# S5's moves between partitions as DMAs, and retention's rotary exchange as a product, in a two-layer hybrid trunk

## The chip, the cores and the metric

The kernel runs on one core of a Trainium2 chip. Its time is the device time of one execution in microseconds. Three runs of the kernel before gave 1293.81 us in the median (1292.19 to 1296.15). The engines are called PE (TensorE), DVE (VectorE), ACT (ScalarE), POOL (GpSimd) and SP (SyncE).

## The reference, cut to what matters

The trunk has two layers. Each normalises the 272 tokens (16 meta tokens and 256 of the input, width 1024), multiplies them by one wide matrix `w_in`, and gives slices of the product to four mixers (retention, S5, SSD, HGRN2). Sigmoid gates merge them; an output projection and a squared-ReLU MLP follow. Two pieces matter here.

```python
def rotary(x):                      # retention's q and k, four heads of 64 channels
    cos, sin = ...                  # angles by token and channel
    x1, x2 = x[..., :half], x[..., half:]
    return jnp.concatenate([x1 * cos - x2 * sin, x1 * sin + x2 * cos], axis=-1)

def s5_mixer(u, ...):               # 32 groups of 16 channels, 64 complex states a group
    uf = u.reshape(bsz, t, S5_GROUPS, S5_GROUP)
    bu_re, bu_im = ...              # group by group, uf times B
    _, _, xr, xi = lax.associative_scan(combine, (a_re, a_im, bu_re, bu_im), axis=1)
    y = ...                         # group by group, real part of C x
    y = y.reshape(bsz, t, BRANCH_WIDTH) + d_skip * u
    y = jax.nn.gelu(y)
    a, gt = jnp.split(y @ glu_w + glu_b, 2, axis=-1)
    return a * jax.nn.sigmoid(gt)
```

## The kernel before

Activations lie with the features on the partitions, as tiles of [128, k, 272 tokens]. The weights come in 336 chunks of 128x1024 float32 (512 KB), in the order of their use, and each chunk is used once. SP loads a chunk (`wst`, L318, three buffers); ACT makes its high part `whi` (L325, three buffers) and DVE the rest, `wlo` (L327, two buffers), both in the float32r format. PE then adds 24 products per chunk (`gemm`, L344, L345 and L347): high weights by high activations, high by low, low by high. So PE can't begin a chunk before ACT, nor finish it before DVE.

Beside that, the engines do the mixers' own work, and the order on each engine is written when the program is built, by a scheduler that simulates the program and picks by ranks of urgency; loads and cuts of chunks rank well ahead of their place. A change to one part therefore moves instructions elsewhere. The order on an engine is fixed at run time: an instruction that waits holds all that stand behind it.

S5 takes its input from four products `proj` in `s5_in`, 128 channels by 272 tokens each. Its states want another layout: 4 interleaved strands of tokens by 32 channels (two groups) on the partitions, and 68 steps along the free dimension. ACT first takes each product out of PSUM into `early` (L1060), and then 16 copies move blocks of 32 partitions by 4x68 elements from one group of 32 partitions to another: odd quadrants on DVE (L1067), even ones on ACT (L1069). `s5_run` does four pairs of groups at a time, four times a layer: products (L1101), rotation and scans on DVE and POOL (L1107 to L1129), products again (L1135, L1138), and the sum Y (L1140). After the second and the fourth of them `s5_out` applies gelu (L1146) and moves half of the channels back in 16 copies of 32x136 (L1152 on DVE, L1154 on ACT). "Half of S5" below means two such passes and their `s5_out`. At the end of `s5` the split into high and low parts follows (L362 on ACT, L364 on DVE).

The passes of S5 stand among the chunks that other mixers need: the first half of layer 0 ends near chunk 51, the second near chunk 58; in layer 1 near chunks 216 and 224. Retention's `ret_in` runs in the same places: q and k out of PSUM (L1475), the tables of cosine and sine loaded in two pieces (L276), then on POOL four multiplications of 32 partitions each that write to the neighbouring 32 (L1482), one of all 128 (L1483), and two adds (L1486, L1487). Values come out in L1492.

Names: `mb`, `mc`, `ma` and `g` are PSUM banks, `S` places in SBUF handed on, `s5a` to `s5g` the S5 parameters in the making (L1003 to L1051), `cst` the constants.

Of the kernel before, what the change touches and what calls it, by code (L numbers as in the profile page):

```python
# [23 lines left out]
# column offsets of w_in  # L24
# [5 lines left out]
# ---------------------------------------------------------------- chunk order  # L30
# One chunk: [128 rows of the contraction, 8 * 128 columns].
# [28 lines left out]
# ---------------------------------------------------------------- small parameters  # L60
# [11 lines left out]
for _name, _w in (("ident", 128), ("ones", 128), ("cen", 128), ("m432", 432), ("he", 1), ("ho", 1), ("le", 1), ("lo", 1),  # L72
                  ("rh", 1), ("rl", 1), ("r1", 1)):
    CONSTS[_name] = (_n, _w)
    _n += _w
# [3 lines left out]
NST, NHI, NLO = 3, 3, 2  # weight chunks in flight: as loaded, high parts, low parts  # L79
PD, PS = 1500, 400  # how far ahead of their place loads and cuts of chunks rank  # L80
HN, FP = 3000, 3000  # ranks of the head norms' scales and of what fills the norms' waits
RES_DVE, RES_END = 6, 6  # tiles of a residual that VectorE takes; the others are GpSimd's
RES_PE = ("mb", "mb", "mc")  # banks of the last residual's tiles that TensorE sums
STORE = ((3, 5), (6, 8), (5, 6))  # the last residual's other tiles, as they are stored
HOLD = 2  # the chunk after a norm whose cut waits for the norm
OK = 4  # from this k on the second column tile waits for the first
HL, EH = (2, 3), (3, 4)  # chunks of a layer's start whose low, high parts wait for the norm's scale
AK, WARM = 5, 14  # where the first norm's sums come in the second chunk; products before the first
LH, LO, LU = (2,), (2,), (2,)  # chunks after a norm that take their low parts last
# [4 lines left out]
def shape_constants():  # L94
# [10 lines left out]
    put("cen", np.eye(128) - 1.0 / 128)  # L105
    t = np.arange(T)
# [6 lines left out]
    # rows of the log-decays, 16 a head: 0..5 for the high parts, 6..11 for the low parts, the other factor being 1 or 0  # L113
# [15 lines left out]
    # rotary tables with the decay of retention: [128, (c | s), (q0 q1 k0 k1), t]  # L129
# [4 lines left out]
    for i in range(2):  # L134
        for q in range(4):
# [3 lines left out]
            for k in range(2):  # L139
                g = (1.0 / up) * 64 ** -0.5 if k else up  # L140
                rot[rows, 0, 2 * k + i] = np.cos(ang).T * g
                # this row feeds the other half: the first half goes to x1*sin, the second to -x2*sin
                sgn = 1.0 if q % 2 == 0 else -1.0
                rot[rows, 1, 2 * k + i] = sgn * np.sin(ang).T * g
# [10 lines left out]
def layout(inp):  # L155
    """Every array the program reads, laid out for it; values only move."""
# [52 lines left out]
    # [layer, (g p), quarter, (b_re b_im c_re c_im), pair, (g j)], zero where the two groups differ  # L209
# [24 lines left out]
class Net:  # L234
# [27 lines left out]
    # ---- small helpers  # L262
    def slot(self, k, shape, dt=F32):
        """one of the 4352-byte places; each is handed on in program order"""
# [7 lines left out]
    def load_after(self, out, in_, dep):  # L272
        """a load that takes its tile only when dep is there"""
# [28 lines left out]
    def behind(self, *key):  # L302
        """a chunk's parts may have to wait their turn on an engine"""
        return self.tc.issue_after(self.hold[key].ins) if key in self.hold else nullcontext()

    # ---- weights: each chunk comes in float32 and is cut into two float32r parts, exactly
# [26 lines left out]
    def gemm(self, out, w, wk, x, xk, n, start=True, stop=True, after=None, late=False):  # L333
        """out += sum over k of W[wk + k]^T x[xk + k], the three products of the parts that count;
        from k = after[0] on behind the instruction after[1]; with late the weights' low part comes last"""
# [23 lines left out]
    def split(self, src, hi, lo, scale=1.0):  # L359
        """hi + lo == scale * src, both float32r."""  # L360
# [15 lines left out]
    def tables(self, name):  # L376
        """the activation tables of what follows, ahead of it"""
        self.tc.keep_in_program_order(self.nc.scalar.preload_act_table_set(name))

    # ---- one layer  # L380
# [4 lines left out]
    def run(self):  # L385
# [4 lines left out]
        # keys, padded with zeros to three tiles of 128 tokens  # L390
# [4 lines left out]
        # the array's clock comes up while the first loads are under way  # L395
# [6 lines left out]
    def layer(self, l):  # L402
# [7 lines left out]
        # ---- pre-mix norm: the first products take h * w as it is, and the norm's scale after them  # L410
# [45 lines left out]
        if not last:  # L456
            # parameters of the next layer's S5, for what the norms leave idle
# [12 lines left out]
        # ---- out projection  # L470
# [15 lines left out]
        # ---- MLP; its input norm's scale s goes into the output's norm: m s^2 / sqrt(mean(m^2 s^4) + eps)  # L486
        # is m / sqrt(mean(m^2) + eps s^-4), and each partition carries its part of the second term
# [36 lines left out]
    def pre_tiles(self, l, wname, sl, big):  # L524
        """h * w, cut in two, as tiles; what makes them and sums the squares of h; and the sums"""
# [34 lines left out]
    def sums_of(self, l, wname, N, mm, extra=None):  # L560
        """products of 8 column tiles, scaled by the norm's weight; and on every partition the sum of their squares"""
# [23 lines left out]
    def fill(self, f):  # L585
        """products between the sums of a norm and what needs it"""
# [3 lines left out]
    def residual(self, mw, ps, sl, fs, eps=True):  # L590
        """h += mw / rms, and what comes next of each tile"""
# [11 lines left out]
        if fs is None:  # L603
            # some of the sums are the tensor engine's, which has h before the norm is there
# [930 lines left out]
```

## Time and profile before

| | |
|---|---|
| median of three runs | 1293.81 us |
| the profiled execution's span | 1294.5 us |
| PE busy | 1231.3 us (95%) |
| DVE busy | 898.3 us (69%) |
| ACT busy | 695.2 us (54%) |
| POOL busy | 388.4 us (30%) |
| DMA | 186.69 MB, 144 GB/s |

PE's share of 95% is the mean over stages that differ: the norms, and the stretch around layer 0's S5, hold most of the idle time. A row of a timeline gives the start in us, the duration, and in brackets how long the engine was idle before and who released it. Two rows may overlap by some tens of ns, since an instruction starts while the one before it drains.

### The profile page before, as it was taken

To read this page: it belongs to the slowest core of one execution; us is meant where nothing else is said; L and a number is where in the kernel's file an instruction comes from. 1 tells how busy PE (TensorE), PEld (TensorE's weight loads), DVE (VectorE), ACT (ScalarE), POOL (GpSimd) and SP (SyncE) were. 2 spreads that over 40 slices of the span, in tenths; PEclk is the share of its full clock that TensorE was granted. 3 is DMA by queue.
4 is the path that set the end of the run, shared out by engine and by line. 5 is a ranking of instruction groups with operands and counts; after the bars stand their busy time and mean duration, and the time that the engine had idled before them with its cause. 6 is when DMAs were issued, how large, how long until landed. Compare 5 with 4: busy or idle time off the path is not lost.

```text
span 1294.5 us, 24278 instructions
## 1 busy us (share of the span) xinstructions
PE 1231.3 (95%) x9534; PEld 1185.8 (92%) x9534; DVE 898.3 (69%) x1480; ACT 695.2 (54%) x1218; POOL 388.4 (30%) x416
## 2 busy tenths in 40 slices
PE   9999998986999989999989999998999998999997
PEld 8989888885999989999988999998999997999996
DVE  8999958987555775554459795689865486655444
ACT  6446755533465466554445548546536456665442
POOL 2332336686100332210015241265680031322001
PEclk9999999997999999999999999998999999999999
DMA  6423332341345435445443332442343554455552
GB/s 238 154 84 114 112 125 94 103 140 65 115 169 174 172 110 183 172 178 175 170 145 131 121 128 83 154 142 92 115 160 131 188 181 153 153 189 183 188 184 98
DMA packets 53187, 186.69 MB, mean 144 GB/s; under 512 B 6096, under 2 KB 7248, under 8 KB 53072
## 3 DMA queue, kind: packets, MB, share of 16 engines
q1 hardware_dynamic: 50480, 179.40, 40.1%
q10 hardware_dynamic: 2592, 5.74, 1.3%
q8 instruction: 75, 1.23, 0.4%
q14 instruction: 40, 0.33, 0.1%
HBM read 184.06 MB, written 1.05 MB: 143 GB/s over the span
## 4 chain that ended last, share of the span: by engine, by line
PE 70%; DVE 17%; POOL 5%; issue 5%; ACT 2%; DMA 1%; DVEq 0%; SPq 0%; ACTq 0%; POOLq 0%
PE g L347 21%; PE g L345 21%; PE g L344 21%; DVE wlo L327 4%; DMA s5a<-in_bc 1%; DVE S L1152 1%; PE mb L711 1%; POOL S L1482 1%; PE mb L717 1%; DVE S L1395 1%; DVE s5a L1004 1%; DVE h L600 1%; DVE S L1262 1%; PE ma L711 1%; PE ma L717 1%
## 5 line engine op out<-in xcount | busy, mean ns | idle before, releaser
L327 DVE TENSOR_TENSOR wlo<-wst,whi 128x1024 fp32r<-128x1024 f32 x336 | 434.5, 1294 | 244.0 <-PE g L347 209.8
L325 ACT ACTIVATE whi<-wst 128x1024 fp32r<-128x1024 f32 x336 | 355.6, 1059 | 368.8 <-PE g L345 285.4
L347 PE MATMUL g<-xh_u,wlo 128*128 128x272 f32 (+1 forms) x1024 | 301.7, 296 | 16.5 <-DVE wlo L327 16.4
L344 PE MATMUL g<-xh_u,whi 128*128 128x272 f32 (+1 forms) x1024 | 300.3, 294 | 1.3 <-ACT S L654 0.9
L345 PE MATMUL g<-xl_u,whi 128*128 128x272 f32 (+1 forms) x1024 | 298.1, 292 | 0.0
L344 PE MATMUL g<-S,whi 128*128 128x272 f32 (+1 forms) x832 | 236.1, 288 | 4.2 <-ACT S L537 3.7
L347 PE MATMUL g<-S,wlo 128*128 128x272 f32 (+1 forms) x808 | 230.5, 289 | 1.8 <-DVE wlo L327 1.8
L345 PE MATMUL g<-S,whi 128*128 128x272 f32 (+1 forms) x768 | 220.4, 289 | 3.1 <-DVE S L548 3.1
L347 PEld LDWEIGHTS g<-xh_u,wlo 128*128 128x128 f32 x1024 | 196.3, 192 | 20.8 <-DVE wlo L327 18.7
L344 PEld LDWEIGHTS g<-xh_u,whi 128*128 128x128 f32 x1024 | 196.9, 192 | 3.4 <-ACT S L654 1.0
L345 PEld LDWEIGHTS g<-xl_u,whi 128*128 128x128 f32 x1024 | 196.8, 192 | 0.8 <-issue 0.4
L344 PEld LDWEIGHTS g<-S,whi 128*128 128x128 f32 x832 | 157.3, 190 | 5.0 <-ACT S L537 4.2
L347 PEld LDWEIGHTS g<-S,wlo 128*128 128x128 f32 x808 | 152.3, 190 | 2.7 <-DVE wlo L327 2.4
L345 PEld LDWEIGHTS g<-S,whi 128*128 128x128 f32 x768 | 146.0, 190 | 4.9 <-DVE S L548 4.7
L345 PE MATMUL g<-xl_npm,whi 128*128 128x272 f32 (+1 forms) x512 | 148.3, 291 | 2.0 <-DVE xl_npm L548 2.0
L344 PE MATMUL g<-xh_npm,whi 128*128 128x272 f32 (+1 forms) x512 | 143.6, 288 | 2.4 <-ACT xh_npm L537 2.4
L347 PE MATMUL g<-xh_npm,wlo 128*128 128x272 f32 (+1 forms) x496 | 142.6, 288 | 0.0
L345 PEld LDWEIGHTS g<-xl_npm,whi 128*128 128x128 f32 x512 | 98.4, 192 | 2.9 <-DVE xl_npm L548 2.6
L673 POOL TENSOR_TENSOR acc<-acc,tmp 128x272 f32<-128x272 f32 (+1 forms) x48 | 38.0, 807 | 205.4 <-DVE tmp L672 205.4
L344 PEld LDWEIGHTS g<-xh_npm,whi 128*128 128x128 f32 x512 | 96.5, 192 | 3.0 <-ACT xh_npm L537 2.9
L347 PEld LDWEIGHTS g<-xh_npm,wlo 128*128 128x128 f32 x496 | 95.0, 192 | 0.2
L503 POOL TENSOR_TENSOR tmp<-tmp 128x272 f32<-128x272 f32 (+1 forms) x64 | 42.1, 658 | 141.1 <-DVE wlo L327 101.0
(379 smaller groups left out, 2194.4 us busy)
## 6 DMA issues: line engine op xcount, KB each, us to landing
wst<-in_w SPq DMA_DIRECT2D x336, 512.0 KB, 3.5
S<-in_rot ACTq DMA_DIRECT2D x4, 544.0 KB, 5.0
s5a<-in_bc ACTq DMA_DIRECT2D x8, 256.0 KB, 3.7
h<-in_h SPq DMA_DIRECT2D x4, 272.0 KB, 4.8
S<-in_ssdc ACTq DMA_DIRECT2D x2, 384.0 KB, 4.4
dtc<-in_ssdc ACTq DMA_DIRECT2D x2, 272.0 KB, 4.7
out<-h SPq DMA_DIRECT2D x2, 256.0 KB, 2.5
S<-in_lvl SPq DMA_DIRECT2D x1, 448.0 KB, 7.7
```

The costliest lines, as they stand in the source:

```text
L325: a = nc.scalar.activation(hi, st, AF.Copy)
L327: nc.vector.tensor_tensor(out=lo, in0=st, in1=hi.bitcast(F32), op=ALU.subtract)
L344: self.nc.tensor.matmul(out, lhsT=a, rhs=r, start=st, stop=False)
L345: self.nc.tensor.matmul(out, lhsT=a, rhs=s, start=False, stop=False)
L347: end = self.nc.tensor.matmul(out, lhsT=b, rhs=r, start=False, stop=en)
L503: nc.gpsimd.tensor_tensor(out=q, in0=a, in1=a, op=ALU.mult)
L600: e.tensor_tensor(out=self.h[:, k, sl], in0=self.h[:, k, sl], in1=mw[:, k], op=ALU.add)
L673: nc.gpsimd.tensor_tensor(out=a, in0=a, in1=t, op=ALU.add)
L711: nc.tensor.matmul(ps[:, c0:c0 + T - q0], lhsT=k[b, 128 * s:128 * s + 128], rhs=q[b, q0:T], start=True, stop=True)
L717: nc.tensor.matmul(out[:, 0:T], lhsT=v01[0], rhs=P[:, 0:272], start=True, stop=False)
L1004: e.tensor_tensor(out=tmp, in0=X[1 - r], in1=F[1], op=ALU.mult)
L1152: nc.vector.tensor_copy(o, i)
```

## The change

The copies of S5 become DMAs on ACT's queue, and `early` and `yf` are laid with the strands outside, so that each DMA has runs of 68 elements (272 bytes). There are 16 in `s5_in` and 16 in each of the two `s5_out` of a layer, so 96 in both layers, in place of 48 copies on DVE and 48 on ACT. The split behind them reads its input with a stride now.

```diff
     def s5_in(self, l, u):
-        uf = self.early[:, 0:4].rearrange("p a (c s) -> p a c s", s=4)
+        uf = self.early[:, 0:4].rearrange("p a (s c) -> p a s c", s=4)
         for i in range(4):
             ps = self.proj(l, O_S5 + 128 * i, u)
-            nc.scalar.activation(uf[:, i], ps.rearrange("p (c s) -> p c s", s=4), AF.Copy)
+            nc.scalar.activation(uf[:, i], ps.rearrange("p (c s) -> p s c", s=4), AF.Copy)
...
         for q in range(4):
             for s in range(4):
-                o, i = W[32 * s:32 * s + 32, :, q, :], uf[32 * q:32 * q + 32, :, :, s]
-                if q % 2:
-                    nc.vector.tensor_copy(o, i)
-                else:
-                    nc.scalar.activation(o, i, AF.Copy)
+                nc.scalar.dma_start(out=W[32 * s:32 * s + 32, :, q, :], in_=uf[32 * q:32 * q + 32, :, s, :])
...
     def s5(self, l, W):
-        yf = self.slot(6, [128, 4, 68, 4])
+        yf = self.slot(6, [128, 4, 4, 68])
...
-            self.split(yf[:, i], gh[:, i], gl[:, i])
+            self.split(yf[:, i], cs(gh[:, i]), cs(gl[:, i]))
...
     def s5_out(self, b, Y, yf):
...
-                o, i = yf[32 * q:32 * q + 32, b:b + 2, :, s], G[32 * s:32 * s + 32, :, q, :]
-                if q % 2:
-                    nc.vector.tensor_copy(o, i)
-                else:
-                    nc.scalar.activation(o, i, AF.Copy)
+                nc.scalar.dma_start(out=yf[32 * q:32 * q + 32, b:b + 2, s, :], in_=G[32 * s:32 * s + 32, :, q, :])
```

In `ret_in` the exchange of the halves of each head becomes a product of PE with a permutation (`swap`, a new 128x128 constant, so `cst` grows from 128x823 to 128x951), DVE multiplies the product by the sine table, whose signs change, and POOL does the rest tile by tile.

```diff
+    put("swap", np.eye(128)[p ^ 32])
...
-                sgn = 1.0 if q % 2 == 0 else -1.0
+                sgn = -1.0 if q % 2 == 0 else 1.0
...
         sw = self.slot(13, [128, 4, T])
-        for q in range(4):
-            a, b = slice(32 * q, 32 * q + 32), slice(32 * (q ^ 1), 32 * (q ^ 1) + 32)
-            g.tensor_tensor(out=sw[b], in0=qk[a], in1=rot[1][a], op=ALU.mult)
-        g.tensor_tensor(out=qk, in0=qk, in1=rot[0], op=ALU.mult)
         qf, k = self.slot(14, [128, 4, T]), self.kpad[1]
         q = qf[:, 0:2]
-        g.tensor_tensor(out=q, in0=qk[:, 0:2], in1=sw[:, 0:2], op=ALU.add)
-        g.tensor_tensor(out=k[:, :, 0:T], in0=qk[:, 2:4], in1=sw[:, 2:4], op=ALU.add)
+        for i in range(4):
+            ps = self.bank()[:, :T]
+            nc.tensor.matmul(ps, lhsT=self.c("swap"), rhs=qk[:, i], start=True, stop=True)
+            nc.vector.tensor_tensor(out=sw[:, i], in0=ps, in1=rot[1][:, i], op=ALU.mult)
+            g.tensor_tensor(out=qk[:, i], in0=qk[:, i], in1=rot[0][:, i], op=ALU.mult)
+            g.tensor_tensor(out=q[:, i] if i < 2 else k[:, i - 2, 0:T], in0=qk[:, i], in1=sw[:, i], op=ALU.add)
```

Comments went too, so that lines before and after differ by a few: L1144 is gelu after, L1148 the moves out, L326 and L328 the cuts.

The scheduler's order changes with it. ACT at the end of layer 0's second half of S5 has before, with `whi_3523` and `whi_3560` the high parts of chunks 59 and 60 (58 was cut ahead of these rows):

```order
277 L362 ACTIVATE S_202_2250<-S_145_1815 128x272 x2
278 L1021 ACTIVATE s5b_2982<-s5a_2973 128x4x32
279 L1021 ACTIVATE s5c_2983<-s5a_2973 128x4x32
280 L1027 ACTIVATE s5c_2983<-s5g_2975 128x128
281 L1146 ACTIVATE S_96_1020<-S_96_1020 128x544
282 L325 ACTIVATE whi_3523<-wst_3521 128x1024
283 L1492 ACTIVATE S_261_3401<-g_3406 128x272
284 L1154 ACTIVATE S_145_1815<-S_96_1020 32x136 x8
285 L325 ACTIVATE whi_3560<-wst_3558 128x1024
286 L1492 ACTIVATE S_261_3401<-g_3444 128x272
287 L362 ACTIVATE S_202_2250<-S_145_1815 128x272 x2
```

and after, where `whi_3498`, `whi_3536`, `whi_3573` and `whi_3611` are chunks 58 to 61:

```order
285 L326 ACTIVATE whi_3498<-wst_3496 128x1024
286 L1469 ACTIVATE S_253_3260<-g_3357 128x272
287 L1144 ACTIVATE S_96_1020<-S_96_1020 128x544
288 L1148 DMA S_145_1815<-S_96_1020 32x2x68 x16
289 L326 ACTIVATE whi_3536<-wst_3534 128x1024
290 L326 ACTIVATE whi_3573<-wst_3571 128x1024
291 L326 ACTIVATE whi_3611<-wst_3609 128x1024
292 L1487 ACTIVATE S_261_3396<-g_3419 128x272
293 L1487 ACTIVATE S_261_3396<-g_3457 128x272
294 L363 ACTIVATE S_202_2250<-S_145_1815 128x272 x2
```

The cut of chunk 59 stood between gelu and the copies and stands behind the sixteen DMAs now, together with those of 60 and 61, and the two evictions that stood between the cuts (L1492, now L1487) follow them.

DVE in the same place has before, with `wlo_3486`, `wlo_3524`, `wlo_3561` the low parts of chunks 58 to 60:

```order
534 L1003 TENSOR_TENSOR s5b_2982<-s5a_2973,s5p 128x4x128
535 L1140 TENSOR_TENSOR S_96_1020<-mb_2219,S_200_2200 128x272
536 L1005 TENSOR_TENSOR s5b_2982<-s5b_2982,s5a_2973 128x4x128
537 L364 TENSOR_TENSOR S_203_2251<-S_145_1815,S_202_2250 128x272 x2
538 L327 TENSOR_TENSOR wlo_3486<-wst_3483,whi_3485 128x1024
539 L1152 COPY S_145_1815<-S_96_1020 32x136 x8
540 L327 TENSOR_TENSOR wlo_3524<-wst_3521,whi_3523 128x1024
541 L364 TENSOR_TENSOR S_203_2251<-S_145_1815,S_202_2250 128x272 x2
542 L327 TENSOR_TENSOR wlo_3561<-wst_3558,whi_3560 128x1024
543 L327 TENSOR_TENSOR wlo_3599<-wst_3596,whi_3598 128x1024
```

and after, where `wlo_3461`, `wlo_3499`, `wlo_3537` and `wlo_3574` are chunks 57 to 60:

```order
533 L1004 TENSOR_TENSOR s5b_2982<-s5a_2973,s5p 128x4x128
534 L1138 TENSOR_TENSOR S_96_1020<-mb_2219,S_200_2200 128x272
535 L1006 TENSOR_TENSOR s5b_2982<-s5b_2982,s5a_2973 128x4x128
536 L328 TENSOR_TENSOR wlo_3461<-wst_3458,whi_3460 128x1024
537 L365 TENSOR_TENSOR S_203_2251<-S_145_1815,S_202_2250 128x272 x2
538 L1480 TENSOR_TENSOR S_260_3395<-ma_3407,S_259_3390 128x272
539 L328 TENSOR_TENSOR wlo_3499<-wst_3496,whi_3498 128x1024
540 L1480 TENSOR_TENSOR S_260_3395<-ma_3412,S_259_3390 128x272
541 L328 TENSOR_TENSOR wlo_3537<-wst_3534,whi_3536 128x1024
542 L328 TENSOR_TENSOR wlo_3574<-wst_3571,whi_3573 128x1024
543 L365 TENSOR_TENSOR S_203_2251<-S_145_1815,S_202_2250 128x272 x2
```

The eight copies between chunk 58 and chunk 59 are gone, chunk 57 has moved behind Y (L1138, before L1140), and two of the four multiplications from the exchange (L1480) stand here.

ACT at the end of layer 1's second half of S5 has before, with `whi_10442`, `whi_10491` and `whi_10529` the high parts of chunks 223 to 225:

```order
841 L325 ACTIVATE whi_10442<-wst_10440 128x1024
842 L1475 ACTIVATE S_770_10341<-g_10343 128x256
843 L325 ACTIVATE whi_10491<-wst_10489 128x1024
844 L362 ACTIVATE S_726_9360<-S_679_8982 128x272 x2
845 L1475 ACTIVATE S_770_10341<-g_10375 128x256
846 L1146 ACTIVATE S_633_8401<-S_633_8401 128x544
847 L1154 ACTIVATE S_679_8982<-S_633_8401 32x136 x8
848 L325 ACTIVATE whi_10529<-wst_10527 128x1024
849 L1475 ACTIVATE S_770_10341<-g_10407 128x272
```

and after, where `whi_10455`, `whi_10517` and `whi_10555` are chunks 223 to 225:

```order
855 L363 ACTIVATE S_730_9373<-S_683_8995 128x272 x2
856 L1144 ACTIVATE S_637_8414<-S_637_8414 128x544
857 L1148 DMA S_683_8995<-S_637_8414 32x2x68 x16
858 L326 ACTIVATE whi_10455<-wst_10453 128x1024
859 L326 ACTIVATE whi_10517<-wst_10515 128x1024
860 L326 ACTIVATE whi_10555<-wst_10553 128x1024
861 L1469 ACTIVATE S_774_10354<-g_10356 128x256
862 L1469 ACTIVATE S_774_10354<-g_10388 128x256
```

All three cuts stand behind the DMAs, where two stood ahead of the copies. The two halves in layer 0 and layer 1 that end earlier change in the same manner: in each, one cut that ran ahead of gelu (chunk 51) or the next one (chunk 216) stands behind the sixteen DMAs and the four L1040 (L1041 after), together with the two cuts after it.

## Rows read from the trace of the kernel before

**Rows 1.** the page's part 1: busy time (share) and instructions of each engine

```profile
PE 1231.3 (95%) x9534; PEld 1185.8 (92%) x9534; DVE 898.3 (69%) x1480; ACT 695.2 (54%) x1218; POOL 388.4 (30%) x416
```

**Rows 2.** PE's timeline: start, duration, engine, line, operation, tiles, count, [idle before <- releaser]

```profile
245.96 0.60 PE L1035 MATMUL mc<-s5c 128*32 128x128 f32 x2 [1.04 <-POOL s5c L1005]
257.82 0.39 PE L347 MATMUL g<-xh_u,wlo 128*128 128x272 f32 x1 [1.70 <-DVE wlo L327]
...
294.23 1.03 PE L694 MATMUL ma<-cst,S 128*128 128x128 f32 x6 [1.26 <-ACT S L1492]
302.17 0.59 PE L347 MATMUL g<-xh_u,wlo 128*128 128x272 f32 x1 [6.45 <-DVE wlo L327]
311.70 0.59 PE L347 MATMUL g<-xh_u,wlo 128*128 128x272 f32 x1 [4.18 <-DVE wlo L327]
...
877.70 1.09 PE L692 MATMUL mb<-cst,s5g 128*128 128x128 f32 x4 [2.17 <-DVE s5g L1005]
```

**Rows 3.** windows: length, busy us (instructions) of each engine, granted clock, DMA share, GB/s

```profile
100.00:125.00 25.00, 24.60 (x192) 23.05 (x190) 24.86 (x59) 17.93 (x39) 5.80 (x5) 1.00 0.30 104
275.00:300.00 25.00, 16.03 (x108) 14.60 (x106) 24.97 (x20) 10.68 (x22) 21.66 (x14) 0.88 0.21 71
300.00:325.00 25.00, 18.65 (x101) 17.03 (x102) 16.71 (x19) 6.15 (x15) 11.81 (x12) 0.71 0.25 86
925.00:950.00 25.00, 24.43 (x194) 23.50 (x194) 19.87 (x25) 15.38 (x31) 13.53 (x7) 1.00 0.37 128
```

**Rows 4.** DVE's timeline around layer 0's second half of S5

```profile
294.75 5.36 DVE L364 TENSOR_TENSOR S<-S,S 128x272 fp32r<-128x272 f32 x2
...
302.14 8.25 DVE L1152 COPY S<-S 32x136 f32<-32x136 f32 x8
310.43 1.23 DVE L327 TENSOR_TENSOR wlo<-wst,whi 128x1024 fp32r<-128x1024 f32 x1
311.57 0.78 DVE L364 TENSOR_TENSOR S<-S,S 128x272 fp32r<-128x272 f32 x2
```

**Rows 5.** POOL's timeline in the same stretch

```profile
288.49 11.31 POOL L1482 TENSOR_TENSOR S<-S,S 32x1088 f32<-32x1088 f32 x4
```

**Rows 6.** one line's instructions each: ns min/median/max, first and last start

```profile
L1152 DVE COPY S<-S x32: 278/286/2434, 241.9 to 935.3; 32x136 f32<-32x136 f32 x32
...
L1069 ACT ACTIVATE S<-early x16: 676/686/703, 116.2 to 787.7; 32x272 f32<-32x272 f32 x16
...
L1067 DVE COPY S<-early x16: 387/395/404, 118.0 to 786.5; 32x272 f32<-32x272 f32 x16
...
L994 ACTq DMA_DIRECT2D s5a<-in_bc x8: 334/334/661, 5.6 to 893.6; - x8
...
DMA to landing us min/median/max: 3.0/3.7/7.6
```

**Rows 7.** PE's timeline at a product of L1452; then two lines' instructions

```profile
196.45 0.62 PE L1452 MATMUL ma<-S,cst 128*128 128x272 f32 x2
196.91 0.60 PE L692 MATMUL mb<-cst,s5g 128*128 128x128 f32 x4
...
L1107 DVE TENSOR_TENSOR S<-mb,s5e x8: 426/428/432, 192.6 to 916.6; 128x272 f32<-128x272 f32 x8
...
L673 POOL TENSOR_TENSOR acc<-acc,tmp x48: 726/766/1721, 321.4 to 1069.4; 128x272 f32<-128x272 f32 x24, 128x256 f32<-128x256 f32 x24
```

**Rows 8.** ACT's timeline around layer 0's first half of S5

```profile
241.15 0.66 ACT L1146 ACTIVATE S<-S 128x544 f32<-128x544 f32 x1
...
245.49 1.06 ACT L325 ACTIVATE whi<-wst 128x1024 fp32r<-128x1024 f32 x1
...
249.22 1.74 ACT L1040 ACTIVATE s5d<-mc 32x512 f32<-32x512 f32 x4 [2.39 <-PE mc L1035]
```

**Rows 9.** ACT's timeline around layer 1's second half of S5

```profile
932.08 3.63 ACT L1154 ACTIVATE S<-S 32x136 f32<-32x136 f32 x8
935.74 1.06 ACT L325 ACTIVATE whi<-wst 128x1024 fp32r<-128x1024 f32 x1
```

More of the change, by code (lines that the diff above doesn't have):

```diff
@@ L71 @@
 _n = 0
-for _name, _w in (("ident", 128), ("ones", 128), ("cen", 128), ("m432", 432), ("he", 1), ("ho", 1), ("le", 1), ("lo", 1),
+for _name, _w in (("ident", 128), ("ones", 128), ("cen", 128), ("swap", 128), ("m432", 432), ("he", 1), ("ho", 1), ("le", 1), ("lo", 1),
                   ("rh", 1), ("rl", 1), ("r1", 1)):
@@ L1084, in s5 @@
                 self.s5_out(b - 1, Y, yf)
-        yf = yf.rearrange("p a c s -> p a (c s)")
+        yf = yf.rearrange("p a s c -> p a c s")
         gh, gl = self.slot(9, [128, 4, T], F32R), self.slot(7, [128, 4, T], F32R)
+        cs = lambda a: a.rearrange("p (c s) -> p c s", s=4)
         for i in range(4):
-            self.split(yf[:, i], gh[:, i], gl[:, i])
+            self.split(yf[:, i], cs(gh[:, i]), cs(gl[:, i]))
         return gh, gl
```

## The prediction

> **What bounds the kernel now.** I read the busy times first. TensorE (PE) works 1231.3 of 1294.5 us [rows 1], so all idle time of the bound engine together is 63.2 us, and an edit is worth what it does to that rest, to the clock under the products, or to the amount of PE work. Next I went through PE's own timeline over the stretches where S5 runs, because the change lies there, and looked at every product that starts behind a gap. In layer 0 the reader sees gaps of 1.04, 1.70, 1.26, 6.45 and 4.18 us [rows 2]. The two long ones end on VectorE's (DVE) cut `wlo` of the weights' low part. Both lie in the stretch from 294 to 312 us, and the table by windows shows what that is: DVE busy 24.97 of 25 us, PE only 16.03 and then 18.65, granted clock 0.88 and 0.71 of full speed [rows 3], that is partly at the lower level, 1.2 GHz. This is the one stage of those read here in which DVE and not PE sets the pace for long. Layer 1's second half of S5 (925 to 950 us) has PE at 24.43 of 25 and full clock [rows 3]: there is nothing to gain there, only to lose. Where S5's input is moved, at 100 to 125 us, DVE is full (24.86) but PE is idle for 0.40 us only.
>
> Then DVE's own timeline says why it is late: two splits (L364) take 5.36 us, where two of the same form take 0.78 at 311.57; eight copies of L1152 take 8.25, and only then comes the next cut, 1.23 [rows 4]. The cut `wlo` that PE waits for at 311.70 stands behind those eight copies. GpSimd (POOL) at the same time runs its four 32x1088 multiplications of L1482 for 11.31 us [rows 5]. A copy of L1152 takes 0.278 us at best, 0.286 in the median and 2.434 at most [rows 6]: DVE is slowed while POOL works.
>
> **The change, part by part.**
>
> *1. Products added.* Four exchange products of fp32, 128x272, per layer, 8 in all. L1452 has that shape with a constant on one side; it starts at 196.45 and the next product starts at 196.91 [rows 7], so 0.46 us of PE each, 8 x 0.46 = +3.7 us. PE is the bound, so I count them whole; where PE would have waited anyway they cost nothing (lower bound 0 for layer 0's four, which lie near the gaps).
>
> *2. Layer 0, second half of S5 and retention (288 to 318 us).* What goes from DVE: eight copies, 8.25 us here [rows 4]; what comes: four multiplications out of PSUM, near L1107's 0.43 each [rows 7], 1.7 us. POOL's work in the way goes from 11.31 us of 32x1088 [rows 5] plus one 128x1088 and two adds to eight 128x272 operations at 0.77 (L673) [rows 7], 6.2 us, in pieces. With that the splits' 5.36 us should come near the 0.78 [rows 4], so wlo comes earlier by more than the copies alone. PE idles here 1.26 + 6.45 + 4.18 = 11.89 us [rows 2]. Not all of it goes, because ACT takes over the moves: after Y, gelu 0.66 [rows 8], then 16 DMA issues, of which one takes 0.334 us alone (L994, median) [rows 6]; the order places the cut whi of chunk 59 behind all sixteen, where it was ahead of the copies. At 0.46 per issue (my choice: from 0.33 up for what an issue waits between two) that is 7.4 us, so whi 59 is done at Y + 0.4 + 0.7 + 7.4 + 1.1 = Y + 9.6 and its wlo at about Y + 10.8. PE has chunks 57 and 58 left then, some 24 products at 0.126 us each (24.43 us over 194 products [rows 3]) = 3.0 us a chunk, with the retention's and S5's own products about 7 us. That leaves a stall of about 3.6 us: gain 11.89 - 3.6 = 8.3 us. Clock: the two windows lose 25 x 0.12 + 25 x 0.29 = 10.3 us of full speed; PE stood idle in 15.3 of the 50 us, so about 30% of that fell on idle time, 7.2 us on work. Half of it comes back with the shorter stall: 3.6. Together **-11.9 us**; bounds -19 (all gaps and all the clock's loss) and -3 (the stall of the sixteen issues is as long as the cut's wait now).
>
> *3. Layer 0, first half (241 to 258 us).* Now gelu, then copies, then one cut (245.49, chunk 52), and only at 249.22 the four L1040 [rows 8]. After: gelu, sixteen issues, four L1040 (1.74), a load, and then cuts 51, 52 and 53 in a row; cut 51, which had run ahead of gelu, is behind them all. Its wlo would come at Y + 0.4 + 0.7 + 7.4 + 1.7 + 0.4 + 1.1 + 1.2 = Y + 12.9, where PE has about 7 us of work: a stall of 6 us in place of 1.04 + 1.70. But 52's cut follows at once, DVE being rid of its copies (16 in each layer's S5 output), where PE waited for it until 257.82 before [rows 2], so that most of this is made up: **+1 us**, bounds -2.7 (both gaps go) and +5 (nothing is made up and the clock falls for a while).
>
> *4. Layer 1, first half.* The same order of instructions; PE's largest gap there is 2.17 us and does not end on a cut [rows 2]. **+1**, bounds -1 and +4.
>
> *5. Layer 1, second half.* Now eight copies take ACT 3.63 us, and whi of chunk 225 follows at 935.74 [rows 9]; cuts 223 and 224 had come before them. After, 223, 224 and 225 all stand behind the sixteen issues: Y + 0.7 + 7.4 to the first of them. PE has no gap to give, so the difference of 7.4 + 0.7 to the work at hand (one chunk, 3.0, and what S5 adds) is paid: **+4**, bounds 0 (Y is that much earlier, since DVE loses 16 copies before it) and +8.
>
> *6. S5's input.* 8 ACT copies of 0.69 and 8 of DVE at 0.395 [rows 6] per layer become 16 issues, 5.3 to 7.4 us of ACT for 5.5, and 3.2 us less for DVE. DVE is full there but PE hardly waits: gain at most 0.4 us; the cuts 27 and 195, now behind the issues, cost at most 2 a layer. **0**, bounds -1 and +4. `cst` grows from 411.5 to 475.5 KB at the start: 0, hidden by the loads of the other operands.
>
> Sum: 3.7 - 11.9 + 1 + 1 + 4 + 0 = -2.2 us. Against the profiled execution, 1294.5 us, which is 0.7 above the median of the runs (1293.81), that is 1292.3 in it and **1291.6** of runs.
>
> One page argues against the change. In "Rules for kernel authors" of the Trainium skill's page "DMA: Bandwidth & Descriptors", many small transfers are to be coalesced, since below 64 KB one pays mostly overhead; the same page ("Anatomy of one DMA", its GpSimd path) puts a fixed part of about 2.0 us on a transfer. The 96 moves are of 17 and 35 KB. The row nearest to that in the trace is L994, whose 256 KB land in 3.0 us at best and 3.7 in the median [rows 6]. If sixteen of them ran one behind the other at the page's figure, a block would last 32 us by estimate; if they overlap, the landing is paid once. By that rule the case is the last rival below; my sum doesn't need it.
>
> **Rivals.**
>
> *A, the relief without a new stall (28%).* Issues stay at 0.33 us, as L994's, so a block is 5.3 us, and DVE's earlier cuts cover it. Then of part 2 all 11.9 us of gaps and 3.6 of clock go, part 3 gains its 2.7, parts 4 to 6 are 0: 3.7 - 15.5 - 2.7 = -14.5, 1280.0 in the profiled one, 1279.3 of runs. For it: a cut and an issue both take ACT only shortly; against: the order puts three cuts behind each block.
>
> *B, ACT starves PE (26%), slower.* Place: the four blocks of sixteen issues in S5's output. Price: an issue that waits for its turn in the queues, above 0.55 us each, is 8.8 us a block. From there a stall of 5 to 6 us stands at each of the four, 4 more than PE's reserve of one chunk covers, and in layer 0's second half only 6 us are gained: 3.7 - 6 + 4 + 4 + 6 + 2 = +13.7, 1308 in the profiled one, 1307.5 of runs. For it: whi and the eviction of products (L654, L1475, L1492) are both ACT's, and behind the block; weights and moves share the same hardware queues' semaphores, so an issue may wait on a weight load. Against: the eight issues of L994 take 0.334 in the median and 0.661 at most [rows 6].
>
> *C, the moves run one behind the other (4%).* At 2 us each the last lands 32 us after the first, the splits wait, and the gates of S5 with them, but these come at the end of the layer, so two blocks of four are free: about +25 us, 1319.
>
> **How the numbers follow.** The measurement tells 0.3%, 3.9 us, from no change. My forecast has 42% and its own range is 1284 to 1298 (bounds of parts 2 to 5 taken half each): -2.2 lies inside the band, its share is 17 faster, 18 same, 7 slower. A gives 27 faster and 1 same, B 24 slower and 2 same, C 4 slower: 44% faster, 21% same, 35% slower. The range for 8 in 10 reaches from A's better half to B's: 1278 to 1308.
>
> **What would show it.** Right: DVE's copies gone, the gaps at 302 and 312 us below 4 us together, granted clock there above 0.9, two splits under 2 us; sixteen issues of ACT in 5 to 8 us; PE 3.7 us busier. B is shown by gaps of PE that end on wlo behind each block of L1148 on ACT, and by issues above 0.5 us; C by landings that grow from the first to the sixteenth. My forecast is wrong if the gaps in layer 0 stay although DVE is idle in them, or if layer 1, where little waits now, loses more than 8 us.

## The result and the profile after

The changed kernel takes 1310.13 us in the median of four runs (1308.74 to 1311.68), against 1293.43 of the kernel before in four runs beside it. The ratio is 1.0128, interval 1.0112 to 1.0144: slower by 16.7 us. The forecast was 1291.6 and its range ended at 1308; the rival with ACT's blocks (B) had 1307.5. The profiled execution's span is 1307.0 us, 12.5 more than that of before, and the readings below explain these 12.5.

Busy times of the profiled execution, first line of the page:

```profile
PE 1234.7 (94%) x9550; PEld 1187.3 (91%) x9550; DVE 864.6 (66%) x1440; ACT 670.8 (51%) x1170; POOL 370.9 (28%) x418
```

Against [rows 1] DVE has 33.7 us less to do, ACT 24.4, POOL 17.5, and PE 3.4 more. All three engines that serve PE are less busy and the kernel is slower, so the sums don't tell it. Issuing a DMA isn't counted as busy, and that is where ACT's time went.

To see where in the program the 12.5 us arise, take the end of the same `wlo` cut in both traces (the n-th instruction of L327 before, of L328 after, counted from 0 as the chunks are):

| stretch, by chunk | end before | end after | lost here | forecast |
|---|---|---|---|---|
| to 24 | 112.7 | 110.9 | -1.8 | 0 |
| 24 to 48, S5's input and parameters, layer 0 | 233.0 | 232.1 | +0.9 | 0 |
| 48 to 56, first half of S5, layer 0 | 283.0 | 285.4 | +3.2 | +1 |
| 56 to 80, second half, retention | 389.5 | 383.6 | -8.3 | -11.9, +1.9 of products |
| 184 to 204, input, layer 1 | 835.6 | 830.9 | +1.3 | 0 |
| 204 to 208 | 850.5 | 849.0 | +3.1 | 0 |
| 208 to 220, first half, layer 1 | 918.7 | 924.9 | +7.7 | +1 |
| 220 to 232, second half, retention | 964.8 | 977.3 | +6.3 | +4, +1.9 of products |

To the end of layer 0's part of the table the kernel has gained 5.9 us; layer 1 then loses 18.4. From chunk 232 to the end the difference stays within 0.7 us of 12.5. PE's own timeline in the two layers (start, duration, line, tiles; in brackets the idle time before and what ended it):

```profile
260.13 0.39 PE L348 MATMUL g<-xh_u,wlo 128*128 128x272 f32 x1 [2.40 <-DVE wlo L328]
...
305.25 1.76 PE L695 MATMUL ma<-cst,S 128*128 128x128 f32 x6 [7.78 <-ACT S L1487]
...
884.32 0.38 PE L345 MATMUL g<-xh_u,whi 128*128 128x256 f32 x1 [2.63 <-ACT S L655]
900.38 0.67 PE L1133 MATMUL mb<-S,s5d 128*128 128x68 f32 x2 [3.03 <-POOL s5e L985]
...
943.78 0.59 PE L345 MATMUL g<-xh_u,whi 128*128 128x272 f32 x1 [7.98 <-ACT S L1469]
```

The gaps of 6.45 and 4.18 us that ended on `wlo` [rows 2] are gone. In their place stand one of 7.78 us in layer 0 and one of 7.98 us in layer 1, where PE had been busy for 24.43 of 25 us [rows 3], and both end on ACT's evictions of finished products out of PSUM (L1487, L1469), not on a cut. The gap of 2.63 us at 884.32 lies ahead of its block, whose first issue begins at 886.76, so it isn't the block's. The windows to those of before (length, busy us of PE, PEld, DVE, ACT, POOL, granted clock, DMA share, GB/s):

```profile
275.00:300.00 25.00, 20.88 (x152) 19.20 (x150) 19.20 (x24) 6.37 (x12) 22.34 (x24) 1.00 0.48 158
300.00:325.00 25.00, 19.75 (x131) 17.57 (x132) 10.01 (x13) 11.37 (x21) 6.04 (x10) 0.86 0.33 109
925.00:950.00 25.00, 17.02 (x126) 16.64 (x126) 9.60 (x12) 9.34 (x15) 1.27 (x2) 0.86 0.37 117
```

In layer 0 PE does more in both windows than before and the granted clock rises from 0.88 and 0.71 to 1.00 and 0.86; DVE is no longer full. In layer 1 PE falls from 24.43 to 17.02 us in its window, and the clock from 1.00 to 0.86, so part of that window is at the lower level of 1.2 GHz: PE had idled for the 7.98 us there.

ACT's timeline at the end of layer 1's second half shows what the evictions waited for:

```profile
929.48 0.64 ACT L1144 ACTIVATE S<-S 128x544 f32<-128x544 f32 x1
930.15 10.31 ACTq L1148 DMA_DIRECT2D S<-S  x16
940.51 2.95 ACT L326 ACTIVATE whi<-wst 128x1024 fp32r<-128x1024 f32 x3 [10.39 <-DMA S<-S]
943.37 0.92 ACT L1469 ACTIVATE S<-g 128x256 f32<-128x256 f32 x3
```

Sixteen issues take 10.31 us, where eight copies had taken 3.63 [rows 9]; three cuts follow, and only then the eviction that PE waits for, 943.37 - 929.48 = 13.9 us after gelu began.

The block of layer 1's first half holds something else. ACT, behind sixteen issues that ran from 886.76 to 898.43:

```profile
898.54 0.59 ACT L1041 ACTIVATE s5d<-mc 32x512 f32<-32x512 f32 x1 [11.81 <-DMA S<-S]
```

The last of the four L1041 ends at 900.28, and the product that reads their tile `s5d` (L1133) begins 0.10 us later at 900.38, behind the gap of 3.03 us; in layer 0 the two are as close, 253.33 and 253.43. The profile puts the gap down to POOL's L985, which was done at 900.20. So what stands behind a block and holds PE can be a cut, an eviction of a weight product, or an eviction for S5 itself.

One line's instructions, the moves of S5's output (ns min, median, max):

```profile
L1148 ACTq DMA_DIRECT2D S<-S x64: 592/607/1717, 240.3 to 939.9; - x64
...
DMA to landing us min/median/max: 1.8/1.9/5.7
```

An issue holds ACT's queue for 0.607 us, with the step to the next 10.31 / 16 = 0.64 us; L994's, which loads from device memory, had held it for 0.334 [rows 6]. The landing is short, 1.9 us in the median. So a move of this kind costs the engine that issues it 0.6 us and holds nobody else for long here.

DVE in the same place of layer 0 as [rows 4]:

```profile
290.65 2.14 DVE L365 TENSOR_TENSOR S<-S,S 128x272 fp32r<-128x272 f32 x2
...
303.05 2.36 DVE L328 TENSOR_TENSOR wlo<-wst,whi 128x1024 fp32r<-128x1024 f32 x2 [8.32 <-ACT whi L326]
```

The two splits take 2.14 us instead of 5.36 and the copies are gone. But DVE then stands idle for 8.32 us for ACT's cut: the wait has moved from DVE to ACT.

### The profile page after: what moved, and what is told of

The parts are those of the page before. It is cut to its first block, busy times and chain, and to the rows that moved or that the text cites. A ratio compares the mean times of both kernels' runs of the same rounds, so it can differ in the third digit from the quotient of the medians.

```text
span 1307.0 us, 24392 instructions
## 1 busy us (share of the span) xinstructions
PE 1234.7 (94%) x9550; PEld 1187.3 (91%) x9550; DVE 864.6 (66%) x1440; ACT 670.8 (51%) x1170; POOL 370.9 (28%) x418
## 4 chain that ended last, share of the span: by engine, by line
PE 69%; DVE 18%; POOL 4%; issue 3%; DMA 2%; ACT 2%; ACTq 2%; DVEq 0%; SPq 0%; POOLq 0%
PE g L345 20%; PE g L348 20%; PE g L346 20%; DVE wlo L328 4%; ACTq L1148 2%; DMA wst<-in_w 1%; DVE s5a L1005 1%; DMA s5a<-in_bc 1%; DVE h L601 1%; PE mb L712 1%; DVE S L1389 1%; ACT whi L326 1%; POOL s5e L980 1%; PE mb L718 1%; DVE xl_npm L549 1%
## 5 line engine op out<-in xcount | busy, mean ns | idle before, releaser
L328 DVE TENSOR_TENSOR wlo<-wst,whi 128x1024 fp32r<-128x1024 f32 x336 | 426.3, 1271 | 270.9 <-PE g L348 223.0
L326 ACT ACTIVATE whi<-wst 128x1024 fp32r<-128x1024 f32 x336 | 354.5, 1059 | 366.7 <-PE g L346 255.6
L345 PE MATMUL g<-xh_u,whi 128*128 128x272 f32 (+1 forms) x1024 | 301.0, 294 | 12.5 <-ACT S L1469 8.0
```

Of the source, the lines that this page charges most:

```text
L326: a = nc.scalar.activation(hi, st, AF.Copy)
L328: nc.vector.tensor_tensor(out=lo, in0=st, in1=hi.bitcast(F32), op=ALU.subtract)
L345: self.nc.tensor.matmul(out, lhsT=a, rhs=r, start=st, stop=False)
```

## The experiments

Theory T: an issue of these moves holds ACT for about 0.65 us, 10.3 us a block, and what stands behind the block on ACT, cuts and evictions both, is what PE waits for. Rivals: R1, the transfers themselves (their queues, their landing); R2, retention's new products. Each run is compared with runs of the kernel before on the same chip (1293.4 to 1294.2 us in the median; the chips differ between some of the runs). Every edit also lets the scheduler lay out the rest anew, so a difference between two runs is not the price of the edited lines alone.

| run | S5's input | S5's output | median us | ratio to before (interval) |
|---|---|---|---|---|
| changed kernel | DMA, ACT | DMA, ACT | 1310.13 | 1.0128 (1.0112 to 1.0144) |
| e1 | copies | copies | 1288.13 | 0.9949 (0.9933 to 0.9964) |
| e2, old retention | DMA, ACT | DMA, ACT | 1310.94 | 1.0122 (1.0104 to 1.0141) |
| e3 | DMA, ACT | copies | 1296.32 | 1.0016 (1.0005 to 1.0027) |
| e4 | DMA, ACT | DMA, SP | 1287.23 | 0.9944 (0.9928 to 0.9960) |
| e5 | copies | DMA, SP | 1281.28 | 0.9897 (0.9879 to 0.9915) |
| e6 | DMA, SP | DMA, SP | 1286.68 | 0.9936 (0.9920 to 0.9951) |
| e7 | DMA, ACT | DMA, ACT, low rank | 1283.62 | 0.9918 (0.9894 to 0.9942) |
| e8 | DMA, ACT | DMA, ACT, from device memory | 1298.56 | 1.0036 (1.0023 to 1.0049) |
| e9 | copies | DMA, ACT, low rank | 1282.28 | 0.9909 (0.9894 to 0.9924) |
| e10 | DMA, ACT, low rank | DMA, ACT, low rank | 1286.10 | 0.9936 (0.9916 to 0.9957) |
| e11 | copies | DMA, SP, low rank | 1283.09 | 0.9917 (0.9902 to 0.9932) |
| e12 | DMA, ACT | half DMA on ACT, half copies on DVE | 1299.40 | 1.0047 (1.0029 to 1.0066) |

**e1, retention's part alone.** `s5_in`, `s5` and `s5_out` are those of before.

> The changed kernel with S5's moves as copies again (before's s5_in, s5 and s5_out); only retention's exchange is new. Theory T (an issue of these DMAs holds ACT for 0.65 us, 10.3 us a block, and cuts and evictions behind it starve PE; retention's part is what made layer 0 shorter): 1283 to 1290 us, layer 0 shorter by 5 to 10 us, layer 1 within 2 us of before plus the four products. Rival R2 (retention's new products and multiplications cost the time): 1300 us or more. Rival R1 (the transfers cost, not their issue) agrees with T here.

Measured 1288.13, within T's range; the end of chunk 72 comes 7.3 us earlier than before, and from there to the end the difference stays between 5.8 and 9.1. R2 falls.

**e2, S5's part alone.**

```diff
-        for i in range(4):
-            ps = self.bank()[:, :T]
-            nc.tensor.matmul(ps, lhsT=self.c("swap"), rhs=qk[:, i], start=True, stop=True)
...
+        for q in range(4):
+            a, b = slice(32 * q, 32 * q + 32), slice(32 * (q ^ 1), 32 * (q ^ 1) + 32)
+            g.tensor_tensor(out=sw[b], in0=qk[a], in1=rot[1][a], op=ALU.mult)
```

> The changed kernel with retention as before (POOL's 32x1088 multiplications, no exchange product); only S5's moves are DMAs. Theory T: 1312 to 1322 us, slower than the changed kernel, layer 1 longer by 14 us or more than before. Rival R2: 1300 us or less.

Measured 1310.94, a little below T's range and not told apart from the changed kernel. S5's moves alone make all of the loss. Retention's part gives 5.7 us when S5 copies (e1) and 0.8, which is within the noise, when it issues. By chunks, it gains 3.8 us in layer 0 (to chunk 80) and loses 3.1 of them by the end; that ACT's blocks take it back is a reading, not a test.

**e3, the output by copies.**

```diff
-                nc.scalar.dma_start(out=yf[32 * q:32 * q + 32, b:b + 2, s, :], in_=G[32 * s:32 * s + 32, :, q, :])
+                o, i = yf[32 * q:32 * q + 32, b:b + 2, s, :], G[32 * s:32 * s + 32, :, q, :]
+                if q % 2:
+                    nc.vector.tensor_copy(o, i)
+                else:
+                    nc.scalar.activation(o, i, AF.Copy)
```

> The changed kernel, where s5_out moves by copies on DVE and ACT again (in the changed layout) and s5_in's 16 DMAs stay. Theory T: the four blocks of sixteen issues are what costs, s5_in's issues stand apart from each other, so 1287 to 1296 us; layer 1 longer than before by at most 6 us. If S5's input were the larger part: 1302 us or more.

Measured 1296.32, at the upper end of T's range. The output's DMAs cost 1310.1 - 1296.3 = 13.8 us against copies, and these copies have a stall of their own: PE waits 8.21 us for a `wlo` at 298.85. To e1 there are 1296.3 - 1288.1 = 8.2 us, which I had not expected to be so large. They aren't the input's DMAs alone, because e3 keeps the changed layout of `early` and `yf` and e1 does not.

**e4, the output issued by SP.**

```diff
-                nc.scalar.dma_start(out=yf[32 * q:32 * q + 32, b:b + 2, s, :], in_=G[32 * s:32 * s + 32, :, q, :])
+                nc.sync.dma_start(out=yf[32 * q:32 * q + 32, b:b + 2, s, :], in_=G[32 * s:32 * s + 32, :, q, :])
```

> The changed kernel, where the 64 DMAs of s5_out are issued by SP instead of ACT; the same transfers. Theory T (ACT's hold): the gaps that end on evictions and cuts of ACT go, 1288 to 1302 us, unless SP, held by gelu's wait, lets weights come late (then waits for wst of 3 us or more appear at the four places). Rival R1 (the transfers or their semaphores): 1305 us or more with the gaps still ending on ACT.

Measured 1287.23: the same 64 transfers from another queue are 22.9 us faster. The gaps that ended on ACT behind the blocks are gone: between 236 and 330 us none is longer than 1.5 us, and in layer 1 none of the gaps above 0.4 us from 850 to 965 us ends on ACT. R1 falls. The moves' line in that trace:

```profile
L1148 SPq DMA_DIRECT2D S<-S x64: 589/594/1100, 241.4 to 930.2; - x64
```

An issue costs SP the same 0.594 us. SP has the room here: in these stretches it only loads weights, three chunks ahead, and its sixteen issues are spread over 12.7 to 15.3 us.

**e5, input by copies, output by SP**: e3's copies, in `s5_in`, with e4's line.

> Retention's exchange as a product, S5's input moved by copies, S5's output by DMAs that SP issues. Theory T: the SP version (1287.2 us) less what the input's sixteen issues on ACT cost there; between the version with copies for all of S5 and the one with copies for the output the input's DMAs cost 8.2 us, so 1278 to 1283. If the input's cost came from what the output's moves left on the engines: 1285 or more.

Measured 1281.28, the fastest of the study, 12.6 us below before. In PE's timeline from 925 to 950 us no gap is left.

**e6, all moves issued by SP.**

> The changed kernel with all 96 moves of S5 issued by SP. Theory T: the input's moves don't hold ACT any more; 1279 to 1287 us, unless their landing is what S5's first products wait for (then as 1287 of the version with only the output on SP, or above).

Measured 1286.68, the upper end of the range and the same as e4. Who issues the input's moves makes no difference that can be told in the whole time; by stretches it does, as the account of step 6 below shows.

**e7, the output's DMAs on ACT at a lower rank.**

```diff
+                with self.tc.high_priority(offset=-1500):
-                nc.scalar.dma_start(out=yf[...], in_=G[...])
+                    nc.scalar.dma_start(out=yf[...], in_=G[...])
```

> The changed kernel with the output's 64 DMAs still on ACT, ranked 1500 lower, so that the scheduler puts cuts and evictions between them (cut 51 after the second of the sixteen, cut 52 after the ninth). Theory T in its narrow form (cuts and evictions that stand behind a whole block are what starves PE): 1292 to 1300 us. If the 0.65 us of ACT per issue count as such, wherever they stand: 1304 or more.

Measured 1283.62, faster than expected. The issues cost what they did, 0.607 us each, on the same engine and queue; only their place on ACT changed, and that is worth 26.5 us. ACT's timeline at the end of layer 0's first half of S5:

```profile
240.41 0.64 ACTq L1149 DMA_DIRECT2D S<-S  x1
...
243.77 1.06 ACT L326 ACTIVATE whi<-wst 128x1024 fp32r<-128x1024 f32 x1 [3.40 <-DVE S L1108]
243.82 1.25 ACTq L1149 DMA_DIRECT2D S<-S  x2
244.74 0.38 ACT L655 ACTIVATE S<-g 128x272 f32<-128x272 f32 x1
245.10 1.91 ACTq L1149 DMA_DIRECT2D S<-S  x3
```

Cuts and evictions pass between the issues, and no gap of PE between 236 and 330 us is longer than 2.0 us. The two windows to compare (columns as above; layer 1's stretch lies 10 us earlier here):

```profile
275.00:300.00 25.00, 22.57 (x165) 20.71 (x164) 21.83 (x24) 10.09 (x20) 22.63 (x20) 1.00 0.38 115
915.00:940.00 25.00, 25.00 (x191) 23.68 (x190) 12.76 (x16) 13.15 (x25) 7.40 (x8) 1.00 0.50 155
```

PE has 22.57 us where before had 16.03 [rows 3], full clock in both, and layer 1 loses 2.8 us from chunk 192 to 228, where the changed kernel lost 18. This separates the two halves of T, as far as a run with a new order of the rest can: it isn't the 10 us of ACT, it is that cuts and evictions stand behind them in one piece.

**e8, the same shape from device memory.** The source of the 64 output moves is a weight array instead of Y; the order on ACT is the changed kernel's.

```diff
+        D = self.io["w"][0][:, 0:544].rearrange("p (a q c) -> p a q c", a=2, q=4)
-                nc.scalar.dma_start(out=yf[...], in_=G[32 * s:32 * s + 32, :, q, :])
+                with self.tc.issue_after(act.ins):
+                    nc.scalar.dma_start(out=yf[...], in_=D[32 * s:32 * s + 32, :, q, :])
```

> The changed kernel, whose 64 output moves read the same shape from a weight array in device memory instead of Y in SBUF (so the gelu of S5 is left out of the result); places and order on ACT are those of the changed kernel. It shows what one issue costs by its source. If a source in SBUF is what makes it 0.61 us: issues of 0.33 to 0.35, blocks of 6 us, and, by theory T, 1296 to 1302 us. If the three dimensions of the pattern make it: 0.61 us again and 1308 to 1312.

```profile
L1150 ACTq DMA_DIRECT2D S<-in_w x64: 318/438/1667, 239.6 to 934.1; - x64
```

The price of an issue falls from 592 to 318 ns at its lowest and from 607 to 438 in the median, so the source in SBUF is part of it and the pattern's dimensions aren't all. But a block still takes 8.1 to 12.0 us, not 6, because issues stand still between two as well. In the block of layer 0's second half one begins at 295.75 and one at 300.37, 1.9 and 2.9 us after the issue before had ended; each has a completion semaphore that a weight load of SP used just before, and begins 0.02 or 0.03 us after that load lands. The issues also don't wait for gelu's end, as they did in the changed kernel. The blocks end 7.9 to 10.4 us after gelu begins, where they ended after 11.0 to 12.4, and PE's gaps behind the second and fourth are 5.18 and 3.60 us instead of 7.78 and 7.98. The time, 1298.56, fits T; as a test of the price alone it is not clean.

**e9, e10 and e11, combinations.** e9: copies in, e7's output. e10: e7's lower rank for input and output. e11: copies in, SP's output at the lower rank.

> Retention's exchange as a product, S5's input by copies, S5's output by ACT's DMAs at the lower rank. Theory T: the low-rank version (1283.6 us) less what the input's DMAs cost (5.9 us on the SP versions, 8.2 on the versions with copies for the output): 1275 to 1280 us. If low rank hides the input's cost too: 1281 to 1285.

> The changed kernel with all 96 DMAs on ACT at the lower rank. If the input's cost is the place of its issues on ACT, ahead of cuts 27 and 195: 1276 to 1281 us. If it comes with the moves whoever issues them (on SP it was the same): 1282 to 1287.

> Input by copies, output by SP's DMAs at the lower rank. SP has no cuts and no evictions to hold, so by theory T the rank matters little there: 1278 to 1284 us, as the version at the usual rank (1281.3).

Measured 1282.28, 1286.10 and 1283.09. e9 missed T's range by 2.3 us: beside the low rank the input's DMAs cost nothing that can be told (1283.62 with them, 1282.28 without). e10 shows that a lower rank doesn't help the input. e5, e7, e9 and e11 overlap in their intervals; which of them is best isn't shown.

**e12, blocks half as long.**

```diff
+                if q % 2:
+                    nc.vector.tensor_copy(o, i)
+                else:
+                    nc.scalar.dma_start(out=o, in_=i)
```

> The changed kernel, where each output block has eight DMAs on ACT (even quadrants) and eight copies on DVE (odd ones): same queue, same kind of issue, the block half as long (about 5.2 us at 0.65). Theory T with a reserve of work on PE of about one to two chunks (3 to 7 us): a block of 5.2 us is nearly covered, 1290 to 1299 us, well under the middle (1303) between no DMAs (1296.3) and sixteen (1310.1). If each issue costs in proportion: 1302 to 1305. If it is the transfers' being there at all: 1307 or more.

Measured 1299.40, just above the range's end and 3.6 us under the middle. ACT, then PE in layer 0's second half:

```profile
293.78 5.13 ACTq L1152 DMA_DIRECT2D S<-S  x8
298.96 2.00 ACT L326 ACTIVATE whi<-wst 128x1024 fp32r<-128x1024 f32 x2 [5.20 <-DMA S<-S]
```

```profile
302.64 0.60 PE L348 MATMUL g<-xh_u,wlo 128*128 128x272 f32 x1 [7.71 <-DVE wlo L328]
```

The block is half as long, 5.13 us, but the copies are back on DVE ahead of a cut, and PE's gap ends on `wlo` again, 7.71 us (8.21 in e3, which has copies alone). In layer 1 no gap after the second block is longer than 0.94 us, where sixteen issues had made 7.98. So a block of 5 us is covered there and one of 10 isn't.

## Why the prediction was wrong

The mechanism that decided was in the prediction, as rival B with 26%. The forecast put too low a price on an issue, followed the wrong instruction behind the block, and had no clock to lose in layer 1. By its steps:

*1, the products.* Forecast +3.7 us; PE is busy 3.4 us more. Near in size, though the busy sum also holds what the clock adds or saves, so it isn't the products alone.

*2, layer 0's second half.* Forecast -11.9, less 1.9 that comes back in products, so -10.0; measured -8.3. That POOL's work slowed DVE there was right in direction: in e1, which changes only retention and keeps the copies, the eight copies take 4.97 us where they took 8.25 [rows 4], the two splits 2.56, and the kernel gains 5.7 us. In the changed kernel the splits fell from 5.36 to 2.14, not below 2 as forecast. The stall that was to remain was put at 3.6 us (the forecast's own 10.8 less 7 gives 3.8) and measured 7.78. The forecast's list of gaps in layer 0 was also not whole: it left out 1.84 us at 223.72, 1.14 at 271.00 and 2.17 at 281.47, of which the last ends just ahead of this stretch.

*3 to 5, the other three blocks.* Forecast +1, +1 and +4, the last with 1.9 of products to come on top; measured +3.2, +7.7 and +6.3. This is the term that failed: "At 0.46 per issue" should have been 0.64 and more, so a block is 10.3 to 11.7 us and not 7.4. The row it was taken from, L994, loads from device memory; the move's source is SBUF, and nothing in the trace before showed such an issue. The prediction gave 0.33 as the lower end and, in rival B, "above 0.55" as the point of decision, and chose 0.46 between them for what an issue waits between two. And the step followed the wrong chain: it ran from the block's end to one cut, Y + 0.7 + 7.4, and asked when its low part would be there. What PE waited for at 305.25 and 943.78 was the eviction of a finished product, which stands behind the block and three cuts more; at 900.38 it was L1041 behind the block. The order of ACT, shown ahead of the prediction, has the evictions so.

*The clock.* The forecast counted on it only in layer 0. In layer 1 the stretch from 740 to 960 us has a mean granted clock of 0.95 where it was 0.98, and the window from 925 to 950 one of 0.86 where it was 1.00. In layer 1's first half (890 to 924.9 us) it is 0.82 where the same stretch before, 884 to 918.7, had 0.95: PE had idled for 3.03 us, and from 900 to 905 us, right behind that gap, the granted clock is 0.50. This is a part of the 7.7 us that the forecast put at nothing. Ahead of the block, gaps of 2.61 and 2.63 us (869.35 and 884.32) stand against 2.17 and 1.27 us before (877.70 and 901.19); what makes them stays open.

*6, the input.* Forecast 0, bounds -1 and +4. e4 against e5 says 5.9 us, e3 against e1 8.2 with the layout in it, e7 against e9 1.3, which can't be told from nothing. So the cost depends on what the output does, and what it consists of is only partly known. In layer 1, from chunk 196 to 208, the kernels that issue the input's moves on ACT lose 2.5 to 5.8 us against before, in all eight runs; with copies it is 0.0, and with SP's issues (e6) 0.3. That part goes with the issues on ACT, though the lower rank didn't help it (e10). In layer 0 e6 falls behind e4, by 2.2 us at chunk 192, and the two are level at the end. The wait for the landing isn't the cause in layer 0: the changed kernel's first product that reads the moved tiles (L1099) begins at 186.7 us, and its moves are issued from 114.2 to 127.1. A gap of about 2.1 us in front of L1036 is there in e3, e4 and e7, and not in e1 or e5; a different place of the S5 parameters on DVE and POOL may be behind it, but e7 has it and is level with e9, so it explains little. The cause in layer 0 stays open.

*The rivals.* B's place was right, and its price (0.55 and more, 8.8 us a block) nearest, though still low. That its 1307.5 is only 2.6 us from the result is partly luck: its terms were off both ways, 6 us gained in layer 0's second half for 8.3, 4 lost in layer 1's first half for 7.7. Of its signs the issues above 0.5 us came, but the longest gaps end on evictions, not on `wlo`. Its reason, issues that wait their turn, doesn't hold in the changed kernel: no output issue begins more than 0.2 us after the one before ends, and only three of the 64 last over 0.75 us. The two longest, 1.43 and 1.72 us, are those during which SP issues a weight load. The rest of the price is the issue itself, 0.607 us from SBUF. That moves and weight loads share semaphores is so, and e8 shows issues that wait for a load by it. C is false: landings stay at 1.9 us in the median and fall to 1.8 at the end of a block; sixteen do not add up.

Size did little for the landing: 17 KB take 1.9 us in the median, 34 KB (L1066) 2.0, 256 KB from device memory 3.7 [rows 6]. The Trainium skill's rule on many small transfers ("DMA: Bandwidth & Descriptors", "Rules for kernel authors") says that under 64 KB one pays mostly overhead, and the trace agrees. The overhead that decided here, though, was the issuing engine's time, 0.6 us each and not overlapped on that engine; the landings overlap.

## What to carry to other kernels

In this kernel a DMA in place of a copy paid only where the issuing queue had nothing urgent behind it. Before such a change, price an issue by a row with the same source (SBUF or device memory), multiply by the block, and follow every instruction behind it, evictions too, to whoever waits; then count the clock that PE loses when it stands idle. With the output's moves in one piece on ACT the kernel was 16.7 us slower than before; with the same moves on SP's queue, or on ACT's with cuts and evictions let through between them, it was 6.6 to 12.6 us faster, 5.7 of which retention gives alone.

## What the runs showed of the hardware

- An issue with its source in SBUF held the queue 0.607 us (ACT) and 0.594 us (SP, e4) in the median; the same shape from device memory (e8) 0.438 us, 0.318 at the least. Twice the size made no difference: 34 KB (L1066) took 0.612 us, 17 KB 0.607.
- Moves of 64 runs of 272 bytes landed in 1.9 us in the median (1.8 to 5.7), the 256 KB loads in 3.7 us [rows 6].
- In these kernels the DMAs of ACT and of SP use the same eight completion semaphores, and in the traces of before, the changed kernel and e8 none of them is issued before the last one with its semaphore has landed: in e8 a move's issue began at 300.37 us, when a weight load had landed at 300.34.
